# First pair of feed-forward row blocks by Strassen's scheme too, and 384 columns of a tail tile on ScalarE and GpSimd

## The chip, the cores and the metric

One core of one Trainium2 chip. The metric is the device time of one execution in microseconds. The kernel before takes 814.76 us, the median of 3 runs (814.73 to 815.66).

## The reference

One decoder layer on x, 512 tokens by 1024, float32. Two token mixers (dilated attention and a state-space model) are projected, gated and summed; then

```
mix_out = mixed @ w_out                                   # 1024 x 1024
h   = layer_norm(ALPHA * x + mix_out, ln1)                # ALPHA = 2 ** 0.25
ff  = (silu(h @ w_ff_gate) * (h @ w_ff_up)) @ w_ff_down   # d_ff = 2816
out = layer_norm(ALPHA * h + ff, ln2)
```

The case plays between `mix_out` and the first feed-forward products. The width 2816 is 22 row blocks of 128 for the gate and as many for the up projection.

## The kernel before

A float32 matrix is split into a high part, rounded to the matmul's input format, and a remainder (`hi`, `lo`); a product is three matmuls: hi by hi, hi by lo, lo by hi (`mm3`, L207 to L210). ScalarE rounds (`act.copy(hi, src)`), VectorE subtracts (`tt(lo, src, hi)`). `tt` (L347) and `stt` (L344) are the element operations of two tensors, on VectorE unless another engine is named.

**Order of the work.** Nothing is reordered at run time: each engine carries out its instructions in the order of the program, and the program is written out by hand. The class `Weights` only chooses which weights are made ready next: it has five slots for a hi and lo pair; `release()` gives back the oldest slot in use and starts the next job (`split`), and a job rounds its operand at once and leaves the subtraction in `w.after`, which the next `flush()` runs. So the weights are made a few products ahead. Loads of 1 MB go out on SP's queue.

**Output projection and first normalization (L1532 to L1559).** The output is made in four tiles of 128 tokens (t = 0 to 3), first columns 0 to 511 of all four, then columns 512 to 1023 tile by tile. After each tile of the second half VectorE adds the residual and takes the statistics (`wo_out`, `bn_aggr`), GpSimd raises the variance to the power -0.5 (`rstd`, L1443), and the tile is normalized. `normalize_shared` does tiles 0 to 2: columns 0 to 511 on VectorE (`norm_first`, `norm_second`), the others by one ScalarE operation and two GpSimd operations of 512 columns (L1469, L1470). Tile 3 is done by VectorE alone (`normalize`). `turn_h(t)` transposes a tile on TensorE (eight 128-column transposes into two banks), ScalarE copies it out twice (plain and rounded), VectorE makes the remainder. Tiles 0 and 1 are turned during tiles 2 and 3 of the projection, tiles 2 and 3 after the first feed-forward steps.

**Feed-forward, plain part (L1574 to L1584, L1673 to L1701).** Two of the 22 row blocks (`NPLAIN`) are multiplied plainly: for each of gate and up, eight k-slices by three passes; half of the tokens first, so that work can begin before tiles 2 and 3 are turned. Their weights are four ordinary splits.

**Feed-forward, Strassen part (L1594 to L1671).** The other 20 row blocks are ten pairs. The 1024 inputs are halved, and the two token halves are the columns, so a pair is a 2 by 2 block product, done with seven products of 24 matmuls at 256 columns instead of eight. Product n of pair j needs a weight operand (`prepare(j, n)`: block 11, 12 or 22 of the weights, or one of the sums s0 and s1 made on VectorE, then hi and lo) and a token form (`forms[n]`; 1, 2 and 3 are blocks of h, 4 to 7 are split sums of blocks). `evict(j, n)` combines the results from PSUM with `snap` copies into four `quarter`s, and `finish_pair` multiplies silu(gate) by up.

**Down projection and tail.** These stay as they are, but for the last row tiles: while the last matmuls of tile 3 run, tile 2 (the third tile, `hn[2]`) is normalized; of its columns 512 to 1023 VectorE does the first 256 (`ends[0]`), ScalarE and GpSimd the other 256 (`ends[1]`, L1934 to L1936). Then GpSimd makes tile 3's power (L1443), VectorE normalizes it, and two queues store it.

The later part of the kernel has `add_remainder`, which makes an operand without VectorE: a GpSimd-queue transfer brings the high part with rounding, ScalarE negates it into `lo`, and a second GpSimd-queue transfer adds the weights to it (L1714, L1715).

Of the kernel before, what the change touches and what calls it, by code (L numbers as in the profile page):

```python
# [16 lines left out]
P = 128  # L17
# [26 lines left out]
N_FF = N_OUT + 8  # L44
NPLAIN = 2
# [128 lines left out]
def emit(ctx, tc, i, out):  # L174
# [94 lines left out]
    for f in range(NPLAIN):  # L269
        w.add(i["w_gu"][f], 8)  # L270
# [1188 lines left out]
    def normalize_shared(z, mv, ln, between=None):  # L1459
# [8 lines left out]
        act.activation(z[:, hi], z[:, hi], AF.Identity, bias=nm, scale=mv[:, 3:4])  # L1468
        pool.tensor_tensor(z[:, hi], z[:, hi], ln[:, 0, hi], op=ALU.mult)  # L1469
        pool.tensor_tensor(z[:, hi], z[:, hi], ln[:, 1, hi], op=ALU.add)  # L1470
# [30 lines left out]
    w.loads[ff_first] = deque((lambda j=j: load_a(j)) for j in (1, 2))  # L1501
# [57 lines left out]
    w.split()  # L1559


    fb = {}
# [11 lines left out]
    def ff_mm(f, e, cs):  # L1574
        if (f, e) not in fb:
            fb[f, e] = bank((2 * f + e) % 8, f"fg{f}{e}")
        ws = w.views[N_FF + 2 * f + e]
        for k in range(KT):
            mm3(fb[f, e][:, cs], (ws[0][:, k, :], ws[1][:, k, :]), kslice(hp_, k, cs), k == 0, k == KT - 1)

    def ff_gate(f):
        th = bt.tile([P, 1024], F32, tag="fth", name=f"fth{f}", bufs=1)[:, 0:512]
        act.activation(th, fb[f, 0], AF.Silu)
        tt(ff_at(f, 1)[:, :, 0, :], *(z.rearrange("p (h t) -> p h t", h=2) for z in (th, fb[f, 1])), ALU.mult)  # L1584
# [5 lines left out]
    ops = {}  # L1590
    for j in (1, 2):
        load_b(j)

    def prepare(j, n):  # L1594
        hi, lo = w.take_slot(f"{j}{n}")
        ops[j, n] = tuple(z.rearrange("p (e k c) -> p e k c", e=2, k=4) for z in (hi, lo))
        a11, a12 = (ra[j][:, 1024 * e : 1024 * e + 1024] for e in range(2))
# [461 lines left out]
```

## Time and profile before

| what | before |
|---|---|
| median of 3 runs | 814.76 us |
| the profiled execution's own time | 815.36 us |
| its span | 813.6 us |
| mean granted TensorE clock | 0.997 |
| TensorE (PE) busy | 802.8 us, 99% |
| VectorE (DVE) busy | 667.4 us, 82% |
| ScalarE (ACT) busy | 411.8 us, 51% |
| GpSimd (POOL) busy | 82.1 us, 10% |
| matmuls | 5584 |

The profile is of one execution. A row of the timeline gives the start in us from the span's start, the duration in us, the engine, the line of the kernel, the operation, and output and input with shape and type; brackets give the idle time of the engine before it and what ended it. A row of the groups gives the same for many instructions: busy time, mean of one in ns, idle time before. Matmuls overlap, so a single one lasts longer than the distance to the next; the chain of waits shows the distances. Spans on GpSimd are rough.

### The profile page before, as it was taken

Reading aid. Unit: us, or ns where it says so; the run is one execution under the profiler, and the core shown is the slowest. Engines: PE = TensorE matmul, PEld = TensorE weight load, DVE = VectorE, ACT = ScalarE, POOL = GpSimd, SP = SyncE. Lnnn points to the kernel's source line nnn. Section 1 sums busy time; section 2 is a strip of 40 time slices with the busy share of each in tenths; the row PEclk is TensorE's granted clock in tenths of the full one; section 3 lists DMA queues with packets and bytes.
Section 4 is the critical chain, followed back from the end, with each engine's and each line's share of the span. In section 5 each row is a group of like instructions: output and inputs, shape, how many; then the busy total and the mean of one; then the engine's idle time right before and its main releaser. Section 6 shows DMA issues by size and latency. Waiting matters only on the chain.

```text
span 813.6 us, 13794 instructions
## 1 busy us (share of the span) xinstructions
PE 802.8 (99%) x5584; PEld 722.4 (89%) x5584; DVE 667.4 (82%) x1061; ACT 411.8 (51%) x607; POOL 82.1 (10%) x100
## 2 busy tenths in 40 slices
PE   9999999999999999999999999999999999999995
PEld 7888888888999999988888899999999999888884
DVE  7977998988788799466796698877777789789986
ACT  6964222546575645874242355455555556555521
POOL 0000002230011333000000410000000000010105
PEclk9999999999999999999999999999999999999998
DMA  8732447895145754741624153332322223674444
GB/s 336 199 113 96 144 156 228 206 198 145 31 113 117 151 100 108 242 183 52 259 104 155 52 184 128 137 123 104 105 104 105 105 104 140 271 148 163 136 126 104
DMA packets 32048, 117.49 MB, mean 144 GB/s; under 512 B 7664, under 2 KB 12528, under 8 KB 22512
## 3 DMA queue, kind: packets, MB, share of 16 engines
q1 hardware_dynamic: 23808, 91.83, 32.7%
q0 software_dynamic: 6544, 23.07, 13.8%
q10 hardware_dynamic: 1632, 1.70, 0.6%
q8 instruction: 44, 0.72, 0.4%
q14 instruction: 20, 0.16, 0.1%
HBM read 100.60 MB, written 9.70 MB: 136 GB/s over the span
## 4 chain that ended last, share of the span: by engine, by line
PE 97%; POOL 1%; DVE 1%; issue 0%; ACT 0%; DVEq 0%; POOLq 0%
PE qx L1265 7%; PE dnx L1809 5%; PE dnz L1809 4%; PE qz L1265 4%; PE pu L620 3%; PE pg L208 3%; PE vx L1221 3%; PE pg L209 3%; PE pg L210 3%; PE dny L1809 2%; PE s L844 2%; PE wo L208 2%; PE wo L209 2%; PE b L209 2%; PE b L208 2%; PE wo L210 2%
## 5 line engine op out<-in xcount | busy, mean ns | idle before, releaser
L1609 ACT CAST whi<-sums 128x1024 fp32r<-128x1024 f32 x40 | 41.9, 1048 | 66.2 <-DVE sums L348 66.2
L202 DVE TENSOR_TENSOR wlo<-raw,whi 128x1024 fp32r<-128x1024 f32 x44 | 54.0, 1230 | 19.7 <-ACT whi L201 19.7
L201 ACT CAST whi<-raw 128x1024 fp32r<-128x1024 f32 x44 | 45.8, 1046 | 18.7 <-PE pk L209 11.3
L348 DVE TENSOR_TENSOR wlo<-sums,whi 128x1024 fp32r<-128x1024 f32 x40 | 48.7, 1219 | 0.0
L1160 ACT CAST whi_q<-rq 128x1024 fp32r<-128x1024 f32 x28 | 29.3, 1051 | 36.1 <-DVE rq L348 25.4
L348 DVE TENSOR_TENSOR wlo_q<-rq,whi_q 128x1024 fp32r<-128x1024 f32 x28 | 34.2, 1220 | 15.5 <-ACT whi_q L1160 15.4
L1809 PE MATMUL dnx<-whi_d,pc 128*128 128x512 f32 (+1 forms) x128 | 38.2, 376 | 0.0
L208 PE MATMUL pg<-x_hi,whi 128*128 128x512 f32 x96 | 37.6, 392 | 0.0
L857 ACT ACTIVATE un<-un,st 128x256 f32<-128x256 f32 (+1 forms) x64 | 30.8, 484 | 13.3 <-DVE st L855 13.3
L209 PE MATMUL pg<-x_lo,whi 128*128 128x512 f32 x96 | 37.4, 390 | 0.0
L210 PE MATMUL pg<-x_hi,wlo 128*128 128x512 f32 x96 | 37.4, 389 | 0.0
L782 POOL DMA_DIRECT2D kq<-qz x32 | 25.3, 1752 | 113.6 <-ACT un L869 72.7
L972 ACT ACTIVATE gt<-pg,bgate 128x512 f32<-128x512 f32 x12 | 8.3, 690 | 41.9 <-PE pg L210 41.8
L1721 ACT CAST whi_d<-dn 128x1024 fp32r<-128x1024 f32 x16 | 16.9, 1053 | 22.9 <-DVE dn L348 11.0
L1809 PEld LDWEIGHTS dnx<-whi_d,pc 128*128 128x128 f32 x128 | 23.6, 188 | 4.4
L1731 POOL DMA_DIRECT2D whi_db<-in_w_dp x3 | 1.7, 574 | 246.1 <-PE dny L1809 242.4
L348 DVE TENSOR_TENSOR wlo<-ra,whi 128x1024 fp32r<-128x1024 f32 x20 | 24.4, 1219 | 0.4 <-ACT whi L1609 0.4
L1809 PE MATMUL dnx<-wlo_d,pc 128*128 128x512 f32 (+1 forms) x64 | 24.1, 376 | 0.0
L1265 PE MATMUL qx<-x23h,whi_q 128*128 128x256 f32 x80 | 23.1, 289 | 0.0
L1265 PE MATMUL qz<-x_hi,whi_q 128*128 128x256 f32 x80 | 22.9, 287 | 0.0
L1265 PE MATMUL qz<-x_hi,wlo_q 128*128 128x256 f32 x80 | 22.6, 283 | 0.0
L1265 PE MATMUL qx<-x23h,wlo_q 128*128 128x256 f32 x80 | 22.6, 283 | 0.0
(849 smaller groups left out, 2963.3 us busy)
## 6 DMA issues: line engine op xcount, KB each, us to landing
raw<-in_w_in SPq DMA_DIRECT2D x12, 1024.0 KB, 5.2
ra<-in_w_gu SPq DMA_DIRECT2D x10, 1024.0 KB, 4.7
rb<-in_w_gu SPq DMA_DIRECT2D x10, 1024.0 KB, 5.0
rq<-in_w_quad SPq DMA_DIRECT2D x16, 512.0 KB, 4.2
dn<-in_w_dq SPq DMA_DIRECT2D x8, 1024.0 KB, 4.9
rv<-in_w_in SPq DMA_DIRECT2D x4, 1024.0 KB, 9.6
kq<-qz POOLq DMA_DIRECT2D x32, 128.0 KB, 5.8
raw<-in_w_br SPq DMA_DIRECT2D x4, 1024.0 KB, 4.8
```

Of the source, the lines that this page charges most:

```text
L201: act.copy(hi, src)
L202: dve.tensor_tensor(lo, src, hi.bitcast(F32), op=ALU.subtract)
L208: pe.matmul(dst, a[0], b[0], start=first, stop=False)
L209: pe.matmul(dst, a[0], b[1], start=False, stop=False)
L210: pe.matmul(dst, a[1], b[0], start=False, stop=last)
L348: eng.tensor_tensor(o, a, b, op=op)
L782: pool.dma_start(dst[32 * q : 32 * q + 32], z[32 * (q ^ 1) : 32 * (q ^ 1) + 32], accum_op=ALU.add)
L857: act.activation(pt, pt, AF.Exp, bias=mneg, scale=-1.0, accum_out=zsum)
L1160: act.copy(hi, src)
L1265: pe.matmul(d[:, 256 * e : 256 * e + 256], p_[:, e, k, :], q_[:, k, :], start=(first and e == k == m == 0), stop=(k == 3 and m == 2), skip ...
L1609: act.copy(hi, src)
L1809: pe.matmul(acc[key][0 if key == "v" else e][:, cs], p_, q_[:, cs], start=(key, e) not in begun, stop=(m == 2), skip_group_check=True)
```

## The change

The plain part goes. The eleven pairs are all done by Strassen's scheme, the new one as pair 0. Its products are interleaved with the first ones of pair 1: (0,1), (0,2), the transposes of tiles 2 and 3, (1,1), (1,2), (0,3), (0,6), (0,5), (0,7), (1,5), (0,4), and then pair 1 and the others as before. Weight operands 1 and 2 of pairs 0 and 1 are made by transfers and ScalarE (`add_remainder`): the high parts are asked for when the first half of the output projection is done, the remainders during tiles 1 and 2 of the second half. Three weight sums of pair 0 (for products 5, 6 and 3) are made by GpSimd ahead of product (0,1), the third in a room of its own (`late_sum`); GpSimd also makes the sums for (0,7), (1,5) and (1,6) and two of the four token sums (h2's first half, h1's second half). Within a product the three passes become the outer loop. Tile 2's first half is normalized before its successor's matmuls in the program, its other half after the transposes of tile 1. In the tail `ends` moves the border from column 768 to 640, so that ScalarE and GpSimd do 384 columns and VectorE 128. The weights' layout drops the plain blocks.

```diff
-N_FF = N_OUT + 8
-NPLAIN = 2
...
-    for f in range(NPLAIN):
-        w.add(i["w_gu"][f], 8)
...
-    w.loads[ff_first] = deque((lambda j=j: load_a(j)) for j in (1, 2))
+    w.loads[ff_first] = deque((lambda j=j: load_a(j)) for j in (0, 1))
+    def quad_sum(j, n, s4, eng):
+        a11, a12 = (ra[j][:, 1024 * e : 1024 * e + 1024] for e in range(2))
+        a21, a22 = (rb[j][:, 1024 * e : 1024 * e + 1024] for e in range(2))
+        s0, s1 = sums[:, 0], sums[:, 1]
+        if n == 5:
+            tt(s0, a21, a22, ALU.add, eng=eng)
+        elif n == 6:
+            tt(s1, s0, a11, ALU.subtract, eng=eng)
+        elif n == 3:
+            tt(s4, a12, s1, ALU.subtract, eng=eng)
+        else:
+            tt(s1, a11, a21, ALU.subtract, eng=eng)
+    def prepare(j, n):
+        hi, lo = w.take_slot(f"{j}{n}")
+        ops[j, n] = tuple(z.rearrange("p (e k c) -> p e k c", e=2, k=4) for z in (hi, lo))
+        if j < 2 and n < 3:
+            src = i["w_gu"][2 * j][:, 1024 * n - 1024 : 1024 * n]
+            pool.dma_start(hi, src)
+            remainders.append(lambda: add_remainder(hi, lo, src))
+            return
...
+        s4 = late_sum if (j, n) == (0, 3) else s0
+        src = {1: a11, 2: a12, 4: a22, 5: s0, 6: s1, 3: s4, 7: s1}[n]
+        if n in (5, 6, 3, 7) and (j or n == 7):
+            quad_sum(j, n, s4, dve if j and (j, n) not in ((1, 5), (1, 6)) else pool)
+        act.copy(hi, src)
+        w.flush()
...
+    order = [(0, 1), (0, 2), (1, 1), (1, 2), (0, 3), (0, 6), (0, 5), (0, 7), (1, 5), (0, 4)]
...
     od = [bank(t, f"wo1{t}") for t in range(NTT)]
     w.release()
+    for _ in range(3):
+        w.split()
     for t in range(NTT):
+        if t == 3:
+            high = normalize_low(hn[2], mvs[2], lnb)
         for n in range(4, 8):
             wo_mm(od[t], n, t)
             if n == (None, None, 6, 5)[t]:
                 turn_h(t - 2)
+        if t in (1, 2):
+            for _ in range(2):
+                remainders.popleft()()
         if t == 3:
-            normalize_shared(hn[2], mvs[2], lnb)
+            high()
...
-            w.split()
...
-        for e in range(2):
-            for k in range(4):
-                c = d[:, 256 * e : 256 * e + 256]
-                for m, (p_, q_) in enumerate(((wh, mh), (wh, ml), (wl, mh))):
+        for m, (p_, q_) in enumerate(((wh, mh), (wh, ml), (wl, mh))):
+            for e in range(2):
+                for k in range(4):
+                    c = d[:, 256 * e : 256 * e + 256]
...
+    w.flush()
+    late_sum = quad[:, 2:4].rearrange("p c e t -> p (c e t)")
+    for n in (5, 6, 3):
+        quad_sum(0, n, late_sum, pool)
+    product(0, 1)
+    evict(0, 1)
+    product(0, 2)
+    for t in (2, 3):
+        turn_h(t)
...
+    tt(h1[:, 0:4], h2[:, 0:4], h1[:, 0:4], ALU.subtract)
+    tt(s2, h2[:, 4:8], h1[:, 0:4], ALU.subtract)
+    tt(h2[:, 0:4], h2[:, 4:8], h2[:, 0:4], ALU.subtract, eng=pool)
+    w.release()
+    for n, z in ((5, h1[:, 0:4]), (6, s2)):
+        act.copy(forms[n][0], z)
+    w.flush()
+    tt(forms[6][1], s2, forms[6][0].bitcast(F32), ALU.subtract)
+    product(1, 1)
+    w.release()
+    tt(h1[:, 4:8], h1[:, 4:8], s2, ALU.subtract, eng=pool)
+    w.flush()
+    tt(t1[1], h1[:, 0:4], t1[0].bitcast(F32), ALU.subtract)
+    product(1, 2)
+    w.release()
+    product(0, 3)
+    split(*forms[7], h2[:, 0:4])
+    product(0, 6)
+    evict(0, 6)
+    w.release()
+    evict(0, 2)
+    w.flush()
+    evict(1, 1)
+    product(0, 5)
+    evict(0, 5)
+    w.release()
+    evict(0, 3)
+    tt(quarter(1), quarter(1), psb[0, "w"], ALU.add)
+    w.flush()
+    split(*forms[4], h1[:, 4:8])
+    step(0, 7)
+    step(1, 5)
+    w.release()
+    step(0, 4)
+    finish_pair(0)
+    evict(1, 2)
+    w.release()
...
-    ends = [slice(512, 768), slice(768, 1024)]
+    ends = [slice(512, 640), slice(640, 1024)]
```

`step(j, n)` is `product`, `evict` and `w.release()`.

More of the change, by code (lines that the diff above doesn't have):

```diff
@@ L1467, in normalize_shared, with high @@
         norm_second(z, mv, ln, lo)
[L1468 to L1470 removed]
+        def high():
+            act.activation(z[:, hi], z[:, hi], AF.Identity, bias=nm, scale=mv[:, 3:4])
+            pool.tensor_tensor(z[:, hi], z[:, hi], ln[:, 0, hi], op=ALU.mult)
+            pool.tensor_tensor(z[:, hi], z[:, hi], ln[:, 1, hi], op=ALU.add)
+        return high
+    def normalize_shared(z, mv, ln, between=None):
+        normalize_low(z, mv, ln, between)()
     bst1 = [bt.tile([P, 2, 6], F32, name=f"bsta{t}", bufs=1) for t in range(NTT)]
@@ L1499, in load_dn, with add_remainder, rest @@
         sp.dma_start(z, i["w_dq"][block, q])
-    w.loads[ff_first] = deque((lambda j=j: load_a(j)) for j in (1, 2))
+    w.loads[ff_first] = deque((lambda j=j: load_a(j)) for j in (0, 1))
+    ops = {}
+    remainders = deque()
+    def add_remainder(hi, lo, src):
+        act.mul(lo, hi.bitcast(F32), -1.0)
+        pool.dma_start(lo, src, accum_op=ALU.add)
+    def quad_sum(j, n, s4, eng):
[18 more added lines that the diff above has]
+            return
+        a11, a12 = (ra[j][:, 1024 * e : 1024 * e + 1024] for e in range(2))
+        a21, a22 = (rb[j][:, 1024 * e : 1024 * e + 1024] if j in rb else None for e in range(2))
+        s0, s1 = (sums[:, e] if n in (5, 6, 3, 7) else None for e in range(2))
+        s4 = late_sum if (j, n) == (0, 3) else s0
[4 more added lines that the diff above has]
+        w.flush()
+        def rest():
+            tt(lo, src, hi.bitcast(F32), ALU.subtract)
+            if n == 7:
+                load_a(j + 2)
+            elif n == 4:
+                load_b(j + 2)
+        w.after = rest
+    order = [(0, 1), (0, 2), (1, 1), (1, 2), (0, 3), (0, 6), (0, 5), (0, 7), (1, 5), (0, 4)]
+    for j in range(1, NPR):
+        order += [(j, 2), (j, 5)] * (j > 1) + [(j, 6), (j, 3), (j, 7)] + [(j + 1, 1)] * (0 < j < NPR - 1) + [(j, 4)]
+    w.jobs[ff_first] = deque((lambda j=j, n=n: prepare(j, n)) for j, n in order)
     def wo_mm(d, n, t):
@@ L1572, in ff_at @@
         return ffs[f // 4][:, :, f % 4 : f % 4 + n, :]
[L1574 to L1584, printed above, removed]
     sums = home(6, "sums").rearrange("p (n c) -> p n c", n=2)
     quad = home(3, "quad").rearrange("p (c e t) -> p c e t", c=4, e=2)
[L1590 to L1591 removed]
+    for j in (0, 1):
         load_b(j)
[L1594 to L1597, printed above, removed]
[L1598 to L1624 removed]
     psb = {}
     def product(j, n):
[L1629 removed]
+        x, y, z = ((0, 1, 4), (2, 3, 5))[j % 2]
         b = {1: x, 2: y, 5: z}.get(n)
         key = {1: "x", 6: "x", 7: "x", 4: "x", 2: "y", 5: "z", 3: "z"}[n]
+        if (j, n) == (0, 3):
+            b, key = 6, "w"
         if b is not None:
@@ L1671, in evict, with step @@
             act.activation(snap["th"], quad[:, :, 0, :], AF.Silu)
-    for n in range(3):
-        ff_mm(n // 2, n % 2, slice(0, 256))
-        if n == 1:
-            turn_h(2)
-            turn_h(3)
+    forms = {n: [hp_[m][n - 1][:, :, 0:256] for m in range(2)] for n in (1, 2)}
+    def step(j, n):
+        product(j, n)
+        evict(j, n)
+        w.release()
[8 more added lines that the diff above has]
+        turn_h(t)
     for t in range(NTT):
@@ L1822, in release_dn @@
         w.release()
-    for j, n in order:
+    for j, n in order[10:]:
         if (j, n) == (NPR - 1, 4):
```

54 lines of the change are left out of this document (6 added, 48 removed).

## The prediction

> **What bounds the kernel now.** I read the page first, then the chain of waits, then the windows view of the stretch that the change rebuilds, and last the timelines of VectorE and GpSimd there.
>
> ```profile
> span 813.6 us, 13794 instructions
> ## 1 busy us (share of the span) xinstructions
> PE 802.8 (99%) x5584; PEld 722.4 (89%) x5584; DVE 667.4 (82%) x1061; ACT 411.8 (51%) x607; POOL 82.1 (10%) x100
> ...
> PE 97%; POOL 1%; DVE 1%; issue 0%; ACT 0%; DVEq 0%; POOLq 0%
> ```
>
> TensorE is busy 99% of the span and is 97% of the chain that ends last. A matmul that goes is worth its whole time, and a wait that TensorE gains costs its whole time. In the stretch from the first feed-forward matmul to the fourth Strassen product of pair 1 the runner-up is close:
>
> ```profile
> core 0: us, PE busy (x) PEld busy (x) DVE busy (x) ACT busy (x) POOL busy (x), PEclk, DMA share, GB/s
> 468.00:501.40 33.40, 33.40 (x260) 32.33 (x259) 31.19 (x36) 17.56 (x23) 3.55 (x3) 1.00 0.45 158
> ```
>
> VectorE works 31.19 of 33.40 us, GpSimd 3.55, at full TensorE clock (1.00). GpSimd looks free. Whether it is free to work beside VectorE decides this case.
>
> **Matmuls removed and added.** The two plain row blocks are four groups (gate and up, two blocks) in eight steps of three passes. The groups view of the stretch and the chain show them:
>
> ```profile
> L208 PE MATMUL fg<-hh,whi 128*128 128x256 f32 x48 | 13.7, 284 | 0.0
> ...
> L208 PE MATMUL fg<-hh,whi 128*128 128x512 f32 x8 | 3.1, 391 | 0.0
> ...
> 501.40 2.88 PE fs1x L1641 x24
> ...
> 705.29 10.88 PE dny L1809 x48
> ```
>
> L209 and L210 issue the second and third pass, as often as L208 the first. The mean per matmul overlaps its neighbours, so I price by spacing in the chain: 2.88/24 = 0.120 us at 256 columns, 10.88/48 = 0.227 us at 512. Removed: 144 x 0.120 + 24 x 0.227 = 22.72 us (three times 48 and three times 8). Added: seven products of 24 at 256 columns, 7 x 2.88 = 20.16 us. Net -2.56 us. Some 0.3 us of gaps around the transposes may go too: laid end to end, the new order would reach the fourth product of pair 1, (1,6), at 498.55 us instead of 501.40, -2.85 us. Running the three passes outermost changes no matmul count; it lets the remainder operand arrive 1.92 us (16 x 0.120) after the product starts.
>
> **Operands by transfer.** Products 1 and 2 of both pairs get their high part by a GpSimd-queue transfer and their remainder by a ScalarE negation and an adding transfer. The kernel already does this later on:
>
> ```profile
> rb<-in_w_gu SPq DMA_DIRECT2D x10, 1024.0 KB, 5.0
> ...
> wlo_db<-in_w_dp POOLq DMA_DIRECT2D x3, 512.0 KB, 7.4
> ...
> L1715 POOL DMA_DIRECT2D wlo_db<-in_w_dp x3 | 2.7, 892 | 5.3 <-ACT wlo_db L1714 5.0 <-DVE wlo_d L348 0.3
> ...
> 468.07 0.28 PE L208 MATMUL fg<-hh,whi 128*128 128x256 f32 x1
> 473.99 1.81 PE hb L1525 x16
> ```
>
> The four high parts are issued during the first half of the output projection, more than 20 us ahead. Remainders (0,1) and (0,2) are issued behind the first row tile's normalization on GpSimd (two issues of 0.89 us, done about 458.5) and land 7.4 us later, at 466; product (0,1), which takes over the start at 468.07, wants its remainder 1.92 us in, at 470. Remainders (1,1) and (1,2) go out about 465.3, land at 473 and are wanted from 477.4, after the sixteen transposes. That cover is 4 us each time, so I cost the transfers at nothing; two 1 MB loads that run beside the later ones could eat it, and then about 2 us would be lost (fourth rival). What queues behind the four issues on GpSimd is the small power operation that each row tile's normalization needs. The second tile's is delayed by 0.2 us. VectorE gives that back, since it no longer splits plain weights there (the 1.48 us row at 455.09, below, is one of four such splits that go).
>
> **What moves.** The third row tile's first half is normalized ahead of the second transposed tile's splits on VectorE; by the layout below these end at 467.9 and 468.6, wanted at 469.0 and 471.9, so it is free, with 1.1 us of cover. Its other half starts on GpSimd at 468.4 and is done at 471.0, wanted at 473.8 by the transposes. On SP's queue the first blocks of pairs 0 and 1 take the place of the plain loads, long ahead; their second blocks wait until TensorE has read the output weights whose room they take (463 and 464) and land 5.0 us later, 469, or some 5 us after that where the two and the remainders share the engines.
>
> **The sums on GpSimd.** Eight 1024-column two-operand operations move to GpSimd before (1,6) can run: three weight sums of pair 0 (into sums 5 and 6 and the late sum for 3), two token sums, and the sums for (0,7), (1,5) and (1,6). The timelines show what such operations do to each other. GpSimd:
>
> ```profile
> 454.19 1.30 POOL L1469 TENSOR_TENSOR hn<-hn,lnb 128x512 f32<-128x512 f32 x1 [1.12 <-ACT hn L1468]
> 455.57 2.15 POOL L1470 TENSOR_TENSOR hn<-hn,lnb 128x512 f32<-128x512 f32 x1
> ...
> 471.19 1.29 POOL L1470 TENSOR_TENSOR hn<-hn,lnb 128x512 f32<-128x512 f32 x1
> ```
>
> VectorE, at the same times and in its steady work:
>
> ```profile
> 455.09 1.48 DVE L202 TENSOR_TENSOR wlo<-raw,whi 128x1024 fp32r<-128x1024 f32 x1 [1.16 <-ACT whi L201]
> ...
> 471.28 1.76 DVE L345 SCALAR_TENSOR_TENSOR hn<-hn,mva,lnb 128x512 f32<-128x512 f32 x1
> ...
> 473.62 1.40 DVE L345 SCALAR_TENSOR_TENSOR hn<-hn,mva,lnb 128x512 f32<-128x512 f32 x2
> ...
> 492.24 1.22 DVE L348 TENSOR_TENSOR sums<-sums,ra 128x1024 f32<-128x1024 f32 x1
> 493.37 1.22 DVE L348 TENSOR_TENSOR wlo<-sums,whi 128x1024 fp32r<-128x1024 f32 x1
> ```
>
> The GpSimd operation of 455.57 takes 2.15 us where its like at 471.19 takes 1.29. The 0.86 us more are, but for 0.14, the time until the VectorE operation that began at 455.09 ended (456.57). That one, 1.48 instead of 1.22, had itself begun beside the GpSimd operation that ended at 455.49. At 471.28 VectorE's operation takes 1.76 us, where two of its likes at 473.62 take 1.40 together; it ends 0.56 us after the GpSimd one that began 0.09 us ahead of it. So two such operations, each with two operands in SBUF, run one after the other, in the order in which they ask. Moving a sum to GpSimd does not take it off VectorE: VectorE stands still for all of it whenever its next two-operand operation comes up.
>
> The price of a 1024-column operation on GpSimd is in no row. Twice the 512-column row is 2.58 us. From below: the 256-column operation in the tail (0.78 us, quoted there) plus three steps of the difference between 256 and 512 columns (1.29 - 0.78 = 0.51) is 2.31 us. I take 2.45, the middle, since both ends are worked from the same rows. On VectorE the same sum costs 1.13 us (493.37 - 492.24). The Trainium skill, page "GPSIMD Engine Reference", section "3.1 Elementwise - side-by-side cycle accounting", gives 4497 ns for 2048 columns; half of it, 2.25 us, is an estimate from that page, and the loss below would be 6.6 us by it instead of 8.2. No row here decides between them.
>
> Now the order. I lay each engine's instructions out in program order, start each when its inputs are there, and let the two engines take turns; VectorE at 1.13 us per 1024 columns and 0.62 to 0.70 per 512, ScalarE at about 1 us per 1024 by this row:
>
> ```profile
> 498.45 1.05 ACT L1609 CAST whi<-sums 128x1024 fp32r<-128x1024 f32 x1 [1.94 <-DVE sums L348]
> ```
>
> VectorE finishes the fourth row tile's statistics at 470.3, the power operation ends at 472.0, and at once GpSimd starts its first sum (472.1 to 474.6). Behind it on VectorE waits the last half of the fourth tile's normalization: its two second steps now alternate with the sums and end at 475.1 and 478.0, where TensorE wants them at 474.6 and 475.1. That is **0.55 + 2.44 us** of waiting before product (1,1); in the profile of before the same transposes run through (473.99, 1.81 us).
>
> The third sum ends at 480.4, VectorE splits the transposed tiles until 482.7 and makes the token sums until 485.1; then GpSimd's two token sums (485.0 to 487.4, 488.4 to 490.8) push the remainder of (0,3) to 488.5 and that of form 6 to 491.8. TensorE wants the first at 486.2 (**2.33 us**), the second at 490.4 (**1.44**, and 0.19 for the next remainder). GpSimd's sum for (0,7) takes 494.0 to 496.5, so form 7 and then the remainder of (0,5) end at 498.6; wanted at 495.9 (**2.78**). The sums for (1,5) and (1,6) delay the remainders of (0,7) and (1,5) by 0.65 each, and 0.04 is left at (0,4). The sum of waits is 11.07 us. Product (1,6) starts at 498.55 + 11.07 = 509.62 instead of 501.40: **+8.2 us**. At 2.31 us per sum it is +7.1, at 2.58 +9.3.
>
> A cross-check by load alone: between 472.1 and 498.55 VectorE has some 18.8 us of two-operand work (4 x 0.67 + 4 x 0.62 + 12 x 1.13) and GpSimd 8 x 2.45 = 19.6, 38.4 together in 26.5 us: 11.9 us too much, close to the 11.07 found step by step. Nothing downstream returns it, since TensorE runs without gaps from (1,6) on.
>
> If the load of the second weight block lands late, and the first sum starts at 475.5, the normalization escapes, but (0,3) waits instead: the same layout then gives 511.70 for (1,6), 2.1 us worse. So my bounds are +7.1 and +11.4.
>
> **The tail.** The third row tile's last quarter moves from 256 to 128 columns on VectorE and from 256 to 384 on ScalarE and GpSimd.
>
> ```profile
> 804.34 0.41 DVE L348 TENSOR_TENSOR hr<-hr,dnv 128x256 f32<-128x256 f32 x1
> ```
>
> ```profile
> 803.20 0.93 POOL L1935 TENSOR_TENSOR hr<-hr,lnb 128x256 f32<-128x256 f32 x1 [0.91 <-ACT hr L1934]
> 804.21 0.78 POOL L1936 TENSOR_TENSOR hr<-hr,lnb 128x256 f32<-128x256 f32 x1
> 805.75 0.98 POOL L1443 TENSOR_TENSOR mvb<-mvb,epsb 128x1 f32<-128x1 f32 x1 [0.75 <-DVE mvb L340]
> ```
>
> VectorE's two short operations, halved, save at most 0.2 us each (half of the 0.41 of a 256-column operation), so the last tile's statistics, late by 0.5 us behind the last matmul, can come 0.4 us sooner. GpSimd's two grow to about 1.04 each (between 0.78 and 1.29) and end about 805.5, just before the power operation at 805.75 needs the engine. If GpSimd's first takes its turn between VectorE's two, nothing is won. Between -0.4 and +0.3 (two longer by 0.26 each, less the 0.2 that they now end early); I take -0.1.
>
> **Sum.** 813.6 + 8.2 - 0.1 = 821.7 us span. The profiled execution took 815.36 us, 1.76 outside its span and 0.60 above the median of 814.76. So 815.36 + 8.1 = 823.5 for such an execution, and **822.9** against the median.
>
> **Rivals.** (a) The sums hide: faster. One mechanism, at the last half of the fourth tile's normalization and the ten remainders: VectorE's operations pass GpSimd's. Then TensorE never waits, -2.85 - 0.1, 811.8 us. For it: 3.55 us of GpSimd work in 33.40, and every transfer has its cover. Against it: the rows at 455 and 471. It decides in part, too: the same layout breaks even when a sum keeps VectorE out for 1.25 us instead of 2.45. (b) That halfway case: GpSimd holds VectorE off for half of an operation, between 1.0 us (-0.8) and 1.8 us (+3.0); about 814.5. Against it: both quoted delays are the rest of the other's operation to within 0.2 us. (c) The change doesn't save matmuls: 168 go and 168 come, and if spacing with three passes outermost were no longer 0.120 us the gain of 2.56 would go; by the row at 501.40 I see no reason, since PEld counts a weight load for every matmul already (5584 of each). On top of the forecast: 825.5. (d) Late transfers, on top of the forecast: 825.
>
> **Chances.** Forecast 0.68, with 819.8 to 826.0 as its own range (+5 where some turns fall better than laid out, +11.4 where the load is late); (a) 0.17; (b) 0.10, of it 0.04 faster, 0.03 the same, 0.03 slower; (c) 0.02, (d) 0.03. A measurement of this kernel tells 0.2% (1.6 us) from no change. Faster 0.21, same 0.04, slower 0.75. The overall range runs from 812.0, which takes in (b) and the upper part of (a), to 826.0.
>
> **What would show it.** Right: TensorE gaps before the last transposes and in (0,3), (0,6), (0,5), put down to VectorE; GpSimd's 1024-column rows at 2.3 to 2.6 us alone and longer beside VectorE; VectorE's second normalization steps above 2 us; TensorE's count unchanged at 5584 and its busy time 2.6 us lower; (1,6) near 509.6. Wrong: 1024-column VectorE rows that stay at 1.22 us while a GpSimd sum runs, or (1,6) before 501. It would also be wrong in its reason if the gaps end on a transfer or on ScalarE.

## The result, and the profile after

The changed kernel takes **826.51 us** (median of four, 826.34 to 826.85); the kernel before, run beside it, 814.87 (814.73 to 815.66). The ratio is 1.0141 (1.0124 to 1.0159): 11.6 us slower. The forecast was 822.9 us, 812.0 to 826.0: the time lies 3.6 us above the forecast and 0.5 us above the end of its range. The direction and the mechanism were right; the loss was sized too small.

The page of the profile after, cut to the rows that answer those of before:

```profile
span 824.2 us, 13839 instructions
## 1 busy us (share of the span) xinstructions
PE 804.6 (98%) x5584; PEld 723.8 (88%) x5584; DVE 679.2 (82%) x1060; ACT 416.6 (51%) x614; POOL 109.5 (13%) x116
...
PE 90%; DVE 6%; POOL 2%; issue 1%; ACT 0%; DVEq 0%; POOLq 0%
```

TensorE was 97% of the chain that ends last and is 90% now; VectorE and GpSimd have come into it. The number of matmuls is unchanged, as forecast. The stretch in which that happens, from the first matmul of product (0,1) to the first of (1,6), in the windows view:

```profile
core 0: us, PE busy (x) PEld busy (x) DVE busy (x) ACT busy (x) POOL busy (x), PEclk, DMA share, GB/s
468.31:511.38 43.07, 34.95 (x259) 33.50 (x258) 42.90 (x32) 18.83 (x25) 26.52 (x11) 0.92 0.41 127
```

Before, 33.4 us of this kind held 31.19 us of VectorE. Now VectorE is busy for 42.90 of 43.07 us with four instructions fewer. It does not do more: its instructions take longer. The timelines of VectorE and GpSimd show that the two engines take turns, and that the one that stands and waits is counted as busy. What they take turns at is called the port below. VectorE:

```profile
467.75 2.38 DVE L344 TENSOR_TENSOR hl<-ht,hh 128x512 fp32r<-128x512 f32 x2
...
471.81 6.95 DVE L341 SCALAR_TENSOR_TENSOR hn<-hn,mva,lnb 128x512 f32<-128x512 f32 x4
478.69 4.65 DVE L344 TENSOR_TENSOR hl<-ht,hh 128x512 fp32r<-128x512 f32 x4
483.26 1.21 DVE L344 TENSOR_TENSOR ht<-ht,ht 128x1024 f32<-128x1024 f32 x1
...
485.65 3.43 DVE L344 TENSOR_TENSOR wlo<-quad,whi 128x1024 fp32r<-128x1024 f32 x1
489.01 3.42 DVE L344 TENSOR_TENSOR t23l<-s,t23h 128x1024 fp32r<-128x1024 f32 x1
...
503.40 0.69 DVE L344 TENSOR_TENSOR quad<-quad,fs0w 128x512 f32<-128x512 f32 x1
...
507.45 0.67 DVE L344 TENSOR_TENSOR quad<-snaps,fs0x 128x512 f32<-128x512 f32 x1
```

GpSimd at the same times:

```profile
468.15 1.43 POOL L1467 TENSOR_TENSOR hn<-hn,lnb 128x512 f32<-128x512 f32 x1 [1.18 <-ACT hn L1466]
...
472.94 2.51 POOL L344 TENSOR_TENSOR sums<-rb 128x1024 f32<-128x1024 f32 x1
...
484.62 3.39 POOL L344 TENSOR_TENSOR ht<-ht 128x1024 f32<-128x1024 f32 x1 [3.64 <-DVE ht L344]
487.96 3.39 POOL L344 TENSOR_TENSOR ht<-ht,s 128x1024 f32<-128x1024 f32 x1
...
502.90 2.40 POOL L344 TENSOR_TENSOR sums<-sums,ra 128x1024 f32<-128x1024 f32 x1 [1.21 <-issue]
```

A 1024-column operation of VectorE takes 1.21 us (483.26) where GpSimd is still, and 3.43 or 3.42 (485.65, 489.01) where a token sum runs: its own time and most of the other's. It is not held up by a result that is missing: the operation of 485.65 needs the third weight sum, done at 480.98, and ScalarE's rounding of it, done at 482.07. GpSimd's sums, 2.40 us undisturbed (502.90) and 2.51 behind the rest of a VectorE operation (472.94), are stretched to 3.39 in the same way. The exception is the row at 503.40: with its second operand in PSUM (the bank fs0w) it takes its ordinary 0.69 us in the middle of the GpSimd sum of 502.90. Where that leaves TensorE:

```profile
476.14 0.63 PE L1581 MATMUL hb<-ident,hn 128*128 128x128 f32 x4 [1.04 <-DVE hn L341]
478.91 1.09 PE L1581 MATMUL hb<-ident,hn 128*128 128x128 f32 x4 [2.14 <-DVE hn L341]
479.65 2.06 PE L1655 MATMUL fs1x<-hh,whi 128*128 128x256 f32 x8
...
489.14 1.22 PE L1655 MATMUL fs0w<-hh,wlo 128*128 128x256 f32 x8 [0.67 <-DVE wlo L344]
...
492.48 1.22 PE L1655 MATMUL fs0x<-t23l,whi 128*128 128x256 f32 x8 [1.17 <-DVE t23l L344]
...
499.23 2.08 PE L1655 MATMUL fs0z<-hh,wlo 128*128 128x256 f32 x8 [2.48 <-DVE wlo L344]
...
508.27 2.14 PE L1655 MATMUL fs0x<-t,whi 128*128 128x256 f32 x16 [0.61 <-DVE quad L344]
...
519.85 1.12 PE L1655 MATMUL fs2x<-hh,whi 128*128 128x256 f32 x8
```

Every wait ends on VectorE, at the places forecast: the last transposes, (0,3), (0,6), (0,5). One more is at (0,4), where the forecast had 0.04 us. Eight matmuls take 2.06 and 2.08 us behind the long waits instead of 1.12 to 1.22, because the granted clock is halved there (columns as in the windows view above):

```profile
474.87:478.28 3.41, 0.86 (x7) 0.42 (x4) 3.41 (x2) 2.96 (x6) 3.27 (x2) 1.00 1.03 309
478.30:481.70 3.40, 2.79 (x13) 2.82 (x14) 3.40 (x3) 1.67 (x3) 2.68 (x1) 0.50 0.97 396
495.35:498.76 3.41, 1.40 (x12) 1.19 (x10) 3.41 (x2) 1.15 (x2) 1.61 (x1) 1.00 0.23 41
498.77:502.18 3.41, 2.95 (x14) 2.95 (x15) 3.41 (x3) 1.43 (x3) 2.38 (x1) 0.50 0.63 267
```

**Where the 11.1 us between the two profiled executions lie** (826.46 less 815.36; the remaining 0.5 of the medians' 11.6 is that before's profiled execution stood 0.49 above its median). Product (2,1) is taken as the end of the stretch, since a delay may be made good between (1,6) and there. Its first matmul before:

```profile
509.88 0.28 PE L1641 MATMUL fs2x<-hh,whi 128*128 128x256 f32 x1
```

From 468.07 (the row quoted in the prediction) that is 41.81 us; now it is 519.85 - 468.31 = 51.54: **+9.73**. Ahead of the stretch lie 0.24 us (468.31 - 468.07). Behind it the operation that prepares the last tile's power operation stands in the chains of waits; before:

```profile
core 0 of [0], span 813.6 us
...
805.51 0.15 DVE mvb L340
```

and after:

```profile
core 0 of [0], span 824.2 us
...
815.52 0.15 DVE mvb L336
```

From (2,1) to it: 295.63 us before, 295.67 after (+0.04, so the tail's edit gave nothing). From it to the end of the span: 8.09 and 8.68 (+0.59). Outside the span: 1.76 and 2.26 (+0.50). The sum of 0.24, 9.73, 0.04, 0.59 and 0.50 is 11.10. Spans are printed to 0.1 us; by the unrounded spans of the two traces (813.58 and 824.24) the last two are 0.65 and 0.43.

### The profile page after: what moved, and what is told of

Its sections match the earlier page's. It is cut to its first block, busy times and chain, and to the rows that moved or that the text cites. A ratio compares the mean times of both kernels' runs of the same rounds, so it can differ in the third digit from the quotient of the medians.

```text
span 824.2 us, 13839 instructions
## 1 busy us (share of the span) xinstructions
PE 804.6 (98%) x5584; PEld 723.8 (88%) x5584; DVE 679.2 (82%) x1060; ACT 416.6 (51%) x614; POOL 109.5 (13%) x116
## 4 chain that ended last, share of the span: by engine, by line
PE 90%; DVE 6%; POOL 2%; issue 1%; ACT 0%; DVEq 0%; POOLq 0%
PE qx L1261 7%; PE dnx L1852 5%; PE dnz L1852 4%; PE qz L1261 4%; PE pu L616 3%; PE pg L206 3%; PE vx L1217 3%; PE pg L207 3%; PE pg L208 3%; PE dny L1852 2%; PE s L840 2%; PE b L208 2%; PE b L207 2%; PE b L206 2%; PE qy L1261 2%; PE o L874 2%
## 5 line engine op out<-in xcount | busy, mean ns | idle before, releaser
L1542 ACT CAST whi<-sums 128x1024 fp32r<-128x1024 f32 x43 | 44.9, 1047 | 59.3 <-DVE sums L344 57.8
L200 DVE TENSOR_TENSOR wlo<-raw,whi 128x1024 fp32r<-128x1024 f32 x40 | 48.7, 1222 | 17.5 <-ACT whi L199 17.5
L344 DVE TENSOR_TENSOR wlo<-sums,whi 128x1024 fp32r<-128x1024 f32 x43 | 55.3, 1287 | 0.0
L199 ACT CAST whi<-raw 128x1024 fp32r<-128x1024 f32 x40 | 41.7, 1048 | 18.2 <-PE pk L207 11.3
L1261 PE MATMUL qz<-x_lo,whi_q 128*128 128x256 f32 x80 | 22.6, 283 | 0.0
```

The source lines that it names most:

```text
L200: dve.tensor_tensor(lo, src, hi.bitcast(F32), op=ALU.subtract)
L344: eng.tensor_tensor(o, a, b, op=op)
L1261: pe.matmul(d[:, 256 * e : 256 * e + 256], p_[:, e, k, :], q_[:, k, :], start=(first and e == k == m == 0), stop=(k == 3 and m == 2), skip ...
```

## The experiments

"Stretch" is the time from the first matmul at 468 (of (0,1), or of the plain blocks in the kernel before) to the first of (2,1), "end" from the preparation of the last power operation to the end of the span, both from the profiled execution; an end is good to 0.05 us, since the span is printed to 0.1. Ratios are to the kernel before, run on the same chip.

| kernel | us | ratio | stretch | end |
|---|---|---|---|---|
| before | 814.87 | 1 | 41.81 | 8.09 |
| changed | 826.51 | 1.0141 (1.0124 to 1.0159) | 51.54 | 8.68 |
| e1, sums on VectorE | 818.78 | 1.0041 (1.0025 to 1.0057) | 44.69 | 8.75 |
| e2, sums of 64 columns | 813.41 | 0.9975 (0.9965 to 0.9985) | 39.37 | 8.69 |
| e3, waits filled | 826.78 | 1.0139 (1.0121 to 1.0156) | 51.66 | 8.71 |
| e4, before with the tail's edit | 815.11 | 1.0005 (0.9996 to 1.0015) | 41.82 | 8.04 |
| e5, unused splits dropped | 824.83 | 1.0122 (1.0104 to 1.0140) | 50.47 | 8.71 |
| e6, pair 0's sums on VectorE | 822.82 | 1.0091 (1.0076 to 1.0106) | 48.78 | 8.74 |
| e7, e1 reordered | 818.51 | 1.0037 (1.0023 to 1.0050) | 44.86 | 8.69 |
| e8, e7 and form 4 by transfer | 818.50 | 1.0046 (1.0029 to 1.0064) | 44.54 | 8.75 |
| e9, operands not by transfer | 825.89 | 1.0135 (1.0119 to 1.0152) | 52.67 | 8.09 |
| e10, eviction of (0,7) first | 825.89 | 1.0134 (1.0119 to 1.0149) | 51.40 | 8.72 |
| e11, before with 8 transfers | 815.92 | 1.0010 (1.0000 to 1.0019) | 41.81 | 8.69 |
| e12, before with 24 transfers | 818.69 | 1.0041 (1.0027 to 1.0055) | 42.35 | 10.06 |

**e1: is it the shared port?**

```
-    tt(h2[:, 0:4], h2[:, 4:8], h2[:, 0:4], ALU.subtract, eng=pool)
+    tt(h2[:, 0:4], h2[:, 4:8], h2[:, 0:4], ALU.subtract)
-    tt(h1[:, 4:8], h1[:, 4:8], s2, ALU.subtract, eng=pool)
+    tt(h1[:, 4:8], h1[:, 4:8], s2, ALU.subtract)
-        quad_sum(0, n, late_sum, pool)
+        quad_sum(0, n, late_sum, dve)
-            quad_sum(j, n, s4, dve if j and (j, n) not in ((1, 5), (1, 6)) else pool)
+            quad_sum(j, n, s4, dve)
```

> All eight sums on VectorE, nothing else changed. Theory (one shared port, operations one after another): a sum takes the port for 1.13 us instead of 2.4, so the port is asked for 8 x 1.3 = 10.4 us less and most of the 9.98 us by which product (1,6) came late comes back: (1,6) near 501 (499.5 to 503 allowed), 816.5 us (815 to 818.5). GpSimd has only its normalization halves left, VectorE's busy time between 468 and (1,6) falls although it does 8 operations more. Rival (VectorE is simply overloaded and GpSimd's sums run beside it): 8 x 1.13 = 9 us more on the engine that is waited for, 830 us or more. Rival (the transfers of the operands are late): no change, 826.5 us, with the same gaps ending on transfers.

818.78 us, 7.7 less than the changed kernel, a little above the expected range, and (1,6) comes at 503.63, also a little late. VectorE does eight operations more and its busy time falls. The windows view from (0,1) to (1,6):

```profile
468.29:503.63 35.34, 31.87 (x258) 30.81 (x256) 35.10 (x40) 17.90 (x24) 3.88 (x3) 1.00 0.49 150
```

It is 35.10 us in 40 instructions, against 42.90 in 32. Taking GpSimd's part away makes the engine that is waited for faster, although it gets the work. A wait for a sum that comes late from GpSimd would be idle time of VectorE in the trace, not busy time, so together with the rows above this shows two engines that hold each other off. So the rival by which VectorE is simply overloaded beside a free GpSimd falls, and the one by late transfers too. But VectorE is still busy for 35.10 of 35.34 us. What remains against the kernel before is VectorE's own load.

**e2: what would the change be worth without the sums?**

```
+        if eng is pool:
+            a11, a12, a21, a22, s0, s1 = (z[:, 0:64] for z in (a11, a12, a21, a22, s0, s1))
+            s4 = s4[:, 0:64]
...
+        if j == 0 or (j, n) in ((1, 5), (1, 6)):
+            src = {5: a22, 6: a11, 3: a12, 7: a11, 4: a22}[n]
...
+    tt(h2[:, 0, 0:64], h2[:, 4, 0:64], h2[:, 0, 0:64], ALU.subtract, eng=pool)
```

(the token sum into h1 is cut likewise, and the sum for (1,3) reads a raw block.)

> The eight GpSimd sums stay on GpSimd but are cut to 64 of their 1024 columns; the operands of the products that used them are split from the raw weight blocks instead, so the products are made with other numbers, at the same instruction counts on TensorE, VectorE and ScalarE. Theory: what costs is the time for which each sum holds the port, so with some 0.4 us per sum instead of 2.4 TensorE hardly waits; (1,6) starts at 498.8 to 500.0 instead of 511.38, and the time is 814 to 815.2 us, as far as what grew outside this stretch (1.1 us) stays. Rival (the transfers or the weight loads are late, or the order of the new program costs TensorE time): 824 us or more, with waits left in (0,3), (0,6) and (0,5).

813.41 us, 0.25% less than before (0.15 to 0.35), and somewhat below the expected 814 to 815.2. TensorE does not wait, at full clock, and GpSimd's eight operations are still there:

```profile
467.76:498.66 30.90, 30.90 (x259) 30.74 (x258) 28.33 (x33) 18.53 (x25) 11.90 (x11) 1.00 0.58 185
```

So it is the length of the sums that costs, and neither the transfers, the loads, nor the new order of passes. By itself this kernel does not separate the hold on the port from a late result, since its products no longer read the sums; the row of 485.65 and e1 do. In the stretch 41.81 - 39.37 = 2.44 us are won, the forecast's 2.56 of matmuls; the 0.3 us of gaps that "may go too" did not come. By the difference to 51.54 the sums cost 12.17 us. The GpSimd rows of this kernel show the queue from the other side:

```profile
472.38 0.46 POOL L344 TENSOR_TENSOR sums<-rb 128x64 f32<-128x64 f32 x1
...
480.17 1.30 POOL L344 TENSOR_TENSOR ht<-ht 128x64 f32<-128x64 f32 x1 [5.87 <-DVE ht L344]
```

The same 64 columns take 0.46 us between two short operations of VectorE (512 columns) and 1.30 where they have to let a 1024-column operation of VectorE pass.

**e3: does the halved clock cost anything?**

```
+            if t == 3:
+                fill(3, 8 + 8 * j)
...
+            if (j, n, m) == (0, 5, 2):
+                fill(7, 18)
```

(`fill(n, count)` issues that many 256-column matmuls into bank n.)

> TensorE runs 24 idle matmuls in the two waits before the last transposes (8 and 16) and 18 ahead of the third pass of (0,5), into banks that nothing reads, so that its two long waits are filled and the granted clock need not fall. Theory (the port's queue sets the pace and TensorE would have waited anyway): the half clock of 478.4 to 481.8 and 498.9 to 502.3 goes, but waits take its place, and (1,6) moves by less than 0.7 us; 825.8 to 827 us. Rival (the clock adds its own loss): two stretches of 3.41 us at half clock cost 1.7 us each, so up to 3.4 us come back: 823.1 to 824.5 us.

826.78 us, the stretch 0.12 us longer: no change. The halving is gone (the windows view, as above, at the same times):

```profile
478.30:481.70 3.40, 3.22 (x28) 3.06 (x27) 3.40 (x3) 1.90 (x3) 2.54 (x1) 1.00 0.94 383
498.77:502.18 3.41, 3.12 (x24) 2.92 (x24) 3.41 (x3) 1.78 (x3) 2.40 (x1) 1.00 0.62 259
```

and the wait in (0,3) has taken its place:

```profile
488.97 1.22 PE L1664 MATMUL fs0w<-hh,wlo 128*128 128x256 f32 x8 [2.01 <-DVE wlo L344]
```

2.01 us instead of 0.67. TensorE at half speed only filled time in which it would have waited for VectorE. The rival is refuted; the queue for the port sets the pace.

**e4: the tail's edit alone**

```
-    ends = [slice(512, 768), slice(768, 1024)]
+    ends = [slice(512, 640), slice(640, 1024)]
```

(in the kernel before.)

> The kernel before with the tail's edit alone (VectorE's piece of the third row tile's last half 128 columns instead of 256). Forecast's step: 0.1 us less, between 0.4 less and 0.3 more; by the profile after, where the last normalization stands as far behind (1,6) as before, 0.0. Rival: the 0.6 us after the last store and the 0.5 us outside the span that grew come with this edit: 1.1 us more.

Ratio 1.0005 (0.9996 to 1.0015): nothing, and the end stays at 8.04 us. The edit neither helps nor makes the longer end.

**e5: work that nobody reads**

```
             act.copy(full, bv)
+            if t > 1 and j == 0:
+                continue
             act.copy(hp_[0][j][:, :, tsl], bv)
             tt(hp_[1][j][:, :, tsl], full, hp_[0][j][:, :, tsl].bitcast(F32), ALU.subtract)
```

> The changed kernel without the rounding and the remainder of the first four 128-row blocks of transposed tiles 2 and 3: with the plain row blocks gone no product reads them, and form 5 is written over them. Two VectorE operations (0.6 us each) and two ScalarE copies (0.5 us each) go; the output is the same. Theory (the queue for the port sets the pace from 472 to 508): what leaves the queue comes back whole, 1.2 us: (1,6) at 510.2 (509.7 to 510.7), 825.3 us (824.7 to 825.8). Rival (the pace is set by the clock or by transfers, and VectorE has room): no change, 826.5 us.

824.83 us, 1.7 less; in the stretch 1.07. A microsecond that leaves VectorE's queue comes back nearly whole, as it must if that queue is the bound. The other 0.6 us are within what the executions of this kernel differ by (824.35 to 827.01). The forecast had laid these splits out as needed work.

**e6: three of the eight sums**

```
-        quad_sum(0, n, late_sum, pool)
+        quad_sum(0, n, late_sum, dve)
```

> Only the three weight sums of pair 0 go back to VectorE; the two token sums and the sums for (0,7), (1,5) and (1,6) stay on GpSimd. Theory (queue for the port): 3 x (2.6 - 1.13) = 4.4 us leave the queue, the normalization runs through, the waits of 1.20 and 2.33 us before the last transposes and the half clock behind them go, and (1,6) comes at 507 to 508.2; 822.2 to 823.4 us, a little over half of what all eight gave (7.73 us). Rival (it is the late half of the normalization alone that counts): nearly all of the 7.7 us come back, 819.5 us or less. Rival (the waits before the transposes are only moved, since the later ones would have come anyway): under 1.5 us, 825 us or more.

822.82 us, as expected: 3.7 of the 7.7 us; 2.76 in the stretch. The normalization runs through, but part of what it gains is lost again in (0,3):

```profile
485.95 1.21 PE L1655 MATMUL fs0w<-hh,wlo 128*128 128x256 f32 x8 [2.72 <-DVE wlo L344]
...
496.04 1.22 PE L1655 MATMUL fs0z<-hh,wlo 128*128 128x256 f32 x8 [2.47 <-DVE wlo L344]
```

Against e1 the token sums and the later sums make the other half of the loss (48.78 - 44.69 = 4.09 us of stretch).

**e7 and e8: can order rescue it?** e7 is e1 and e5 with VectorE's program reordered; its core:

```
     w.flush()
-    tt(h2[:, 0:4], h2[:, 4:8], h2[:, 0:4], ALU.subtract, eng=pool)
...
     product(1, 2)
     w.release()
+    w.flush()
+    tt(h2[:, 0:4], h2[:, 4:8], h2[:, 0:4], ALU.subtract)
     product(0, 3)
...
     evict(0, 5)
     w.release()
+    evict(0, 2)
...
+    product(0, 7)
+    evict(0, 7)
...
     evict(0, 3)
     tt(quarter(1), quarter(1), psb[0, "w"], ALU.add)
...
-    step(0, 7)
     step(1, 5)
```

> All eight sums on VectorE, the unused rounding and remainders dropped, and VectorE's order in the stretch changed so that the remainders that TensorE wants first come first: the remainders of (0,3), (0,6) and (0,5) ahead of the token sums for forms 7 and 4 and of the sum for (0,7); the second addition into the quarter of (0,3) after the sum for (1,5). From 818.8 us: the splits give 1.2, the order most of the three waits of 1.83, 0.43 and 1.57 us, but VectorE stays busy without a break, so that part of them comes back at (0,4) and (1,6): (1,6) at 500.5 to 502, 816 us (814.5 to 817). Rival (VectorE's load alone decides, not its order): 817.6 us.

e8 makes the remainder of form 4 by a transfer, and puts the token sum for it back behind product (1,1) (against e7):

```
+    tt(h1[:, 4:8], h1[:, 4:8], s2, ALU.subtract)
+    act.copy(forms[4][0], h1[:, 4:8])
+    add_remainder(*forms[4], h1[:, 4:8])
...
-    tt(h1[:, 4:8], h1[:, 4:8], s2, ALU.subtract)
-    act.copy(forms[4][0], h1[:, 4:8])
...
-    tt(forms[4][1], h1[:, 4:8], forms[4][0].bitcast(F32), ALU.subtract)
```

> As the one before, and the remainder of form 4 is made by a ScalarE negation and an adding transfer on GpSimd's queue, issued behind (1,1), some 12 us ahead of its use. One 1024-column operation, 1.13 us, leaves VectorE; an adding transfer lands in 7 to 9 us by the rows of the changed kernel. Theory: 0.5 to 1.1 us better than the one before, 815 us (813.5 to 816.5). Rival: the transfer lands after (0,4) wants it, and the time is that of the one before or worse.

818.51 and 818.50 us: both expectations missed, no better than e1, though e7 does 1.2 us less on VectorE and e8 2.3 less. The remainders are no longer late; the sums are, and the waits have moved to the rounded high parts made from them. The transfer of e8 is not late: no wait of e8 ends on it. In e7:

```profile
502.23 1.21 PE L1659 MATMUL fs1x<-t23h,whi 128*128 128x256 f32 x8 [2.17 <-ACT whi L1544]
```

A sum needs ScalarE's rounding behind it before TensorE can start at all, a remainder is wanted only in the third pass; putting the remainders first delays the longer chain. That is read from where the waits end. What a best order would give was not found. None of the runs that compute the whole result beats the kernel before.

**e9: the transfers**

```
-        if j < 2 and n < 3:
-            src = i["w_gu"][2 * j][:, 1024 * n - 1024 : 1024 * n]
-            pool.dma_start(hi, src)
-            remainders.append(lambda: add_remainder(hi, lo, src))
-            return
...
-        if t in (1, 2):
-            for _ in range(2):
-                remainders.popleft()()
...
+            w.split()
```

(with the calls that prepare operands spread over the row tiles again.)

> The operands of products 1 and 2 of both pairs are rounded on ScalarE and their remainders taken on VectorE, from the weight blocks already in SBUF, as the plain blocks were; the eight GpSimd-queue transfers (four high parts, four adding ones) go. Forecast's step: the transfers cost nothing, so nothing is to be had by leaving them out; VectorE gets 4 x 1.13 us back in the stretch from 455 to 470, where the kernel before had as much without a gap on TensorE. (1,6) stays at 511.4 within 0.7, 825.8 to 827.2 us. Rival (late transfers): 824.5 us or less. A second question: the time from the last tile's power operation to the end of the span is 8.7 us in the changed kernel and in every kernel run here that has the new pair, and 8.1 us in the kernel before. If the added transfers cause it, it is 8.1 us again and 0.6 us come back.

825.89 us, 0.6 less, within the expectation. Making operands 1 and 2 on the engines lengthens the stretch by 1.13 us, so the transfers were worth having there; late transfers are no part of the loss. The time is shorter all the same, because in the profiled execution the first product starts 0.85 us earlier (467.46), the time outside the span is 0.5 us less, and the end is back at 8.09 us:

```profile
core 0 of [0], span 823.9 us
...
815.81 0.15 DVE mvb L336
```

**e11 and e12: what a transfer on GpSimd's queue costs at the end**

```
+        if 1 < j < 10 and n in (5,):
+            pool.dma_start(spare[j - 2, n], i["w_gu"][2 * j][:, 0:1024])
```

(in the kernel before; e12 has `(5, 3, 7)`.)

> The kernel before with eight more transfers of 512 KB on GpSimd's queue, one in each of pairs 2 to 9, from a weight block to a place in DRAM that nothing reads. Theory from the last run (8.09 us from the last tile's power input to the end of the span without the added transfers, 8.7 with them): each transfer on this queue adds some 0.08 us behind the last store, so 8.7 us here and 815.6 us (815.0 to 816.3). Rival (the end grew for another reason, such as the adding form of the transfer or the new program's length): 8.1 us and no change.

> As the one before with 24 transfers, three in each of the pairs 2 to 9. Theory: it goes by the number of transfers, 8.1 + 24 x 0.08 = 10.0 us from the power input to the end of the span, 816.9 us. Rival (a step by some threshold, not by number): 8.7 us as with eight. Rival (no effect): 8.1 us.

The end is 8.69 us with eight and 10.06 with 24; by 0.08 us each, 8.7 and 10.0 were expected:

```profile
core 0 of [0], span 815.7 us
...
805.64 0.15 DVE mvb L340
```

It goes by number, not by threshold. By the unrounded spans of the traces the end is 8.06 or 8.07 us without added transfers (before, e4, e9), 8.72 with eight (e11 and the changed kernel), 8.80 with nine (e8, which has one more) and 10.02 with 24. e12's median, 3.6 us above before, is more than the 2.0 us of its longer end; 0.54 of the rest lie in the stretch and 0.3 outside the span, and the profiled execution was the fastest of the five, 0.9 us below their median.

**e10: the wait in (0,4)**

```
-    split(*forms[4], h1[:, 4:8])
+    act.copy(forms[4][0], h1[:, 4:8])
     step(0, 7)
+    tt(forms[4][1], h1[:, 4:8], forms[4][0].bitcast(F32), ALU.subtract)
```

> The remainder of form 4 moves on VectorE from before the eviction of (0,7) to behind it; nothing else. Product (0,4) gathers in the bank that this eviction reads, and in the changed kernel waits 0.86 us for it, which the forecast's layout had left out. Theory: the eviction comes 1.1 us earlier, (0,4) loses that wait, its second pass finds the remainder of form 4 just in time: (1,6) at 510.4 to 510.9, 825.5 to 826.0 us. Rival (VectorE's queue sets the end anyway, the wait moves to the remainder of form 4 or of (0,4)): no change, 826.5 us.

825.89 us, 0.6 less. The time is in the theory's range, but not for its reason alone. (0,4) no longer waits, and (1,6) comes 0.85 us sooner behind the first product (42.05 us by its first matmul instead of 42.90), as the theory said. But now (1,7) waits, for ScalarE's copy of (1,6), which it is given behind other copies:

```profile
515.93 1.22 PE L1655 MATMUL fs1x<-t23h,whi 128*128 128x256 f32 x8 [0.45 <-ACT snaps L1677]
```

So the stretch to (2,1) is only 0.14 us shorter. The 0.6 us of the medians is not explained by it: the first product started 0.8 us earlier in this profiled execution than in the changed kernel's, and kernels that are the same up to there differ by as much (467.5 to 468.3).

## Where the prediction went wrong: the mechanism held, the sum was too small

**What it rested on held.** One port, one operation after another, in the order asked: shown by the rows of 3.4 us, whose inputs were ready, by e1 (work put onto VectorE makes VectorE faster) and by e2 (shorter sums, no waits). The price of a sum was taken at 2.45 us; undisturbed rows give 2.38 and 2.40, and 2.51 where a VectorE operation still ran at the start. The Trainium skill, page "SBUF — State Buffer", section "🔬 SBUF: two separate sides", says that the pair of ports which the two engines share is an exclusive lock, held by whoever starts first for the whole instruction; the trace agrees (3.43 us at 485.65 beside 1.21 at 483.26). Its page "GPSIMD Engine Reference", section "3.1 Elementwise - side-by-side cycle accounting", gives 4497 ns for 2048 columns, from which the prediction estimated 2.25 us for a sum; the rows are 0.13 to 0.26 above it.

**By the forecast's own places.** The table gives the waits in the timeline of TensorE, start to start less the normal spacing. In the changed kernel some of them are hidden in matmuls at half clock; e3, whose clock does not fall, shows all of them (its idle matmuls count as waiting):

| place | forecast | changed kernel | e3 |
|---|---|---|---|
| before the last transposes | 0.55 + 2.44 | 1.20 + 2.33 | 1.23 + 2.28 |
| (0,3) | 2.33 | 0.83 | 2.17 |
| (0,6) and the next remainder | 1.44 + 0.19 | 1.33 + 0.18 | 1.31 + 0.18 |
| (0,5) | 2.78 | 2.64 | 2.64 |
| (0,7) and (1,5) | 0.65 each | none | 0.66 each |
| (0,4) | 0.04 | 0.86 | 0.86 |
| sum | 11.07 | 9.37 | 11.99 |

The last three of e3:

```profile
502.68 1.22 PE L1664 MATMUL fs0x<-t23h,wlo 128*128 128x256 f32 x8 [0.50 <-DVE wlo L344]
...
506.32 1.22 PE L1664 MATMUL fs1z<-hh,wlo 128*128 128x256 f32 x8 [0.50 <-DVE wlo L344]
508.14 2.14 PE L1664 MATMUL fs0x<-t,whi 128*128 128x256 f32 x16 [0.60 <-DVE quad L344]
```

So the layout was right to within 0.2 us at every place but the first, 0.68 too small, and the last, 0.82 too small.

**The step that failed is the sum**, "813.6 + 8.2 - 0.1 = 821.7 us span" and "1.76 outside its span": its main terms were right in sign, and each term on the side of the loss was too small or put at nothing:

- "The sum of waits is 11.07 us": 12.17 measured (51.54 less the 39.37 of e2). Two places of the table make it more, by 1.50 us together; the others are 0.58 less. At (0,4) the layout left out that this product gathers in the bank that the eviction of (0,7) reads, and that eviction stands on VectorE behind remainders held up by sums (507.45); in e10, where it comes earlier, the wait is gone. At the transposes, "at once GpSimd starts its first sum (472.1 to 474.6)": it started at 472.94. At 468.15 GpSimd's half of tile 2's normalization came shortly before the second of VectorE's two splits and went first; the two took 2.38 us (467.75) instead of some 1.2, and all behind came later. The forecast's layout had GpSimd come at 468.4, behind VectorE. This second cause is read from the rows, not tested by a run. The rough cross-check by load, 11.9 us, was the nearer one.
- The matmuls: 2.44 us less instead of 2.85. The forecast's own spacings give 2.56, and no row stood behind the 0.3 us of gaps that it added.
- "I cost the transfers at nothing": in the stretch they were worth 1.1 us (e9), but each adds 0.08 us behind the last store (e8, e9, e11, e12); measured +0.59.
- The time outside the span, taken as unchanged at 1.76 us: +0.50. It belongs to the program: 2.24 to 2.26 us in all four executions of the changed kernel, 2.18 to 2.26 in e3, e5 and e10, 1.73 to 1.84 in those of the kernel before. Without the transfers (e9) it is back at 1.73 to 1.75, but so it is with the transfers kept and all or three of the sums on VectorE (e1, e6: 1.75 to 1.82). What is done in that time stays open.
- Ahead of the stretch 0.24, within what executions differ by; the tail +0.04 instead of -0.1 (e4: nothing).

Together 1.10 + 0.41 + 0.59 + 0.50 + 0.24 + 0.14 = 2.98 us, the difference between 8.1 and 11.10. The remaining 0.6 of the 3.6 us is a correction that did not recur: the forecast took off 0.60 because the profiled execution of before stood so far above its median, and that of the changed kernel stood 0.05 below. The stretch, +9.73, lies inside the forecast's own bounds of +7.1 and +11.4. What carried the time beyond 826.0 are the terms outside the stretch and this correction, for which the range had no room.

**Two sentences of "what would show it" were wrong.** TensorE's busy time was to be 2.6 us lower; it is 1.8 higher, since half-speed matmuls count as busy (in e2, where none run at half speed, it is 799.9, 2.9 lower). And (1,6) was to come near 509.6; it came at 511.4. The clock had not been considered at all; that it cost nothing here was luck of the bound.

**The rivals.** (a) sums that hide and (b) half a hold fell with e1 and the 3.4 us rows. (c), dearer passes, fell with e2, whose stretch is shorter by the saving in matmuls with the passes outermost. (d), late transfers, fell with e9. The load of the second weight block, whose lateness made the upper bound of 11.4, was not late: the first sum starts as the power operation ends. The chances of the forecast and (a) to (d) add up to 0.03 for the same and 0.76 for slower, where it says 0.04 and 0.75.

## What to carry to other kernels

An engine with 3.55 us of work in 33.40 is not free: ask what it shares. Moving a sum from VectorE to GpSimd cost 0.86 us of the stretch each here (51.54 - 44.69 over eight), and with all eight left on VectorE they still cost 5.32 (44.69 - 39.37), more than the 2.44 us of matmuls that the change bought, since VectorE was 31 of 33 us full already. Before pricing a rewrite by its matmuls, add up what its operands cost on the runner-up engine, and look for work that the rewrite leaves without a reader (e5).

## What the runs showed of the hardware

- **The clock is granted by a fixed grid.** Halvings begin at 478.29 and 498.77 in the changed kernel, 20.48 us apart, six times the 3.413 us that each lasts; in e5 one lasts two steps. What TensorE did in the step before goes with it, though not by one clean line. In the stretches of the changed kernel and the runs, every step with 0.37 to 1.40 us of TensorE work in its 3.41 was followed by half clock, every one with 1.66 or more (e8) by full clock. Between the two it went both ways: behind 1.52 (e7) and 1.64 us (e5) the clock was halved, behind 1.49 (e9) and 1.58 us (e3) it was not. The step ahead of the first halving in e5, and the step of e9 behind which the clock stayed full, in the windows views of the two:

```profile
481.09:484.51 3.42, 1.64 (x14) 1.43 (x13) 3.38 (x3) 2.13 (x3) 2.20 (x2) 1.00 0.10 42
```

```profile
476.16:479.57 3.41, 1.49 (x13) 1.52 (x14) 3.41 (x2) 1.72 (x4) 3.33 (x2) 1.00 0.24 101
```

  The length of a wait does not decide either: in e6 waits of 2.72 and 2.47 us (rows above) passed at full clock, while in e7 one of 2.17 us halved it. The stretch of e6, and two steps of e7:

```profile
467.91:508.05 40.14, 32.19 (x257) 30.87 (x256) 39.90 (x35) 18.57 (x25) 18.70 (x8) 1.00 0.44 134
```

```profile
500.35:503.75 3.40, 1.52 (x12) 1.52 (x13) 3.33 (x4) 2.41 (x3) 0.00 (x0) 1.00 0.67 277
503.76:507.17 3.41, 3.41 (x18) 3.41 (x17) 2.96 (x3) 3.38 (x5) 0.00 (x0) 0.50 0.38 101
```

  The Trainium skill, page "TensorE: Matmul & The Clock Gate", section "🔬 Part 1: The HAM clock gate (the "warmup" mystery)", gives a free-running window of 3413 ns, which agrees; by it the clock falls after an idle window, where here a window in which TensorE was busy for about half was enough in some cases (1.64 of 3.41 us in e5).
- **Transfers on GpSimd's queue are paid for at the end of the program**: 0.08 us for each, all of 512 KB here, long after those of the changed kernel have been read by its products. Eight and 24 of them into memory that nothing reads lengthen the time behind the last power operation by 0.60 and 1.97 us. What is done in that time no row of the profile shows.
- **A PSUM operand passes.** VectorE's addition with one operand in PSUM runs at its ordinary 0.69 us beside a GpSimd sum (503.40 beside 502.90 in the changed kernel; 0.67 at 507.45, where GpSimd is still).
